# A hybrid encoder layer on one core: where the sigmoids of r and ga and the attention's heads are placed in the weight stream

## Chip, core and metric

The kernel runs on one core of one Trainium2 chip. The metric is the device time of one execution in microseconds; for a program on one core that is the time of this core. The times shown are those of three runs. The profile is of one execution.

## What is computed

One layer: a token mixer and a channel mixer, each with a norm ahead, a norm behind, and scale, shift and gain from a conditioning vector. There are 256 tokens and 2048 features, all in float32. The part that matters here is the token mixer:

```python
def token_mixer(h, w_in, w_a2, b_a2, gla_norm_g, w_out_gla, conv_mix_w, w_out_conv, w_o):
    q, k, v, r, lr, cb, cc, cx, ga, gb = jnp.split(h @ w_in, split_idx, axis=-1)
    log_a = jax.nn.log_sigmoid((lr @ w_a2 + b_a2).astype(jnp.float32)) / GLA_TAU
    o = gla_chunked(heads(q, GLA_DK) * (GLA_DK ** -0.5), heads(k, GLA_DK),
                    heads(v, GLA_DV), heads(log_a, GLA_DK))
    o = rmsnorm(o, gla_norm_g).astype(h.dtype).reshape(bsz, s, GLA_V)
    y_a = (o * jax.nn.silu(r)) @ w_out_gla
    y_b = (cb * causal_dwconv(cc * cx, conv_mix_w)) @ w_out_conv
    m = jax.nn.sigmoid(ga) * y_a + jax.nn.sigmoid(gb) * y_b
    return m @ w_o
```

`gla_chunked` is a linear attention with 4 heads over 4 chunks of 64 frames: a state for each head is decayed by the low-rank gate `log_a` and added to, and every frame reads the state behind its chunk.

## The kernel before

**The weight stream.** All large products go through one list of items, `stream`. A `Chunk` is 256 rows by 512 columns of a weight: one DMA of 512 KB into a buffer `raw` (6 buffers, L275), a rounded copy `whi` on ScalarE (L282, ACT in the profile), the rest `wlo` on VectorE (L291, DVE), and products on TensorE (PE) of `whi` with both parts of the activations and of `wlo` with the high part. In `Feat` (features on partitions, L345) a chunk is 24 matmuls with 256 columns: 16 with `whi`, 8 with `wlo`. A `Gemv` is one tile of 128 x 1024 of `w_ada`, loaded into the same buffers and added to a partial sum on DVE (L438); it uses no PE. `pump(n)` writes out n items of the stream: loads up to 10 items ahead, splits up to 4 ahead, then the item's products. With `each=step_bg` it also runs the generator `bg` one step further behind each `Chunk`, and `run_all(bg)` writes out what is left of it at once.

**Order of execution.** What the program writes out is a text of instructions. The framework then orders the instructions of each engine by a model of the time: the earlier place in the text has the higher priority, but an engine that would be idle in the model takes a later instruction that is ready, and a tile gets a buffer of its tag when one is free (`t2` has 4 buffers, `c4` 2, `g8` 4, the PSUM banks `sm` 2). On the chip each engine then goes through its list in that order.

**The stages around the change**, in the order of the stream, with Gemv items spread between the chunks:

- the last slice of `w_in`'s early columns, `r` among them;
- `cb1` (8 chunks of `w_in`), whose outputs go through `post_cb` (L645, then L633 and L634) into `yb`;
- `w_out_conv` (4 groups of 4 chunks), which reads `yb`; `post_yb` (L653) multiplies by sigmoid(gb);
- `ga` (4 groups of 8 chunks of `w_in`); `post_ga` copies each group to `ga_t` (L677);
- `w_out_gla` (4 groups of 4 chunks), which reads the heads' results `og`, chunk i of a group that of head i; `post_ya` (L806, L807, L633, L634) multiplies by sigmoid(ga) and adds the other branch;
- `w_o` (4 groups of 8 chunks, L400), then the middle of the layer and the channel mixer.

**Background steps beside them.** `gla_gates` runs beside `cb1` and `w_out_conv`, 24 chunks together. It has 21 steps: 4 sigmoids of gb (L662), the split of the low-rank weights (L694, L695), four steps of their product (L699, L700), its copy (L706), two of `w_a2` (L712), log-sigmoid (L716 to L721), the decays of k (L727 to L730), idle ones, and the decay of each chunk of frames, `dtot` (fold, L741, L743). `w_a2` and the low-rank weights each lie in a `t2` buffer from the start to their product.

`gla_heads` runs beside `ga`, 32 chunks. It has 4 steps of SiLU of r (`silus`: sigmoid into a `t2` buffer, L669, and product, L670) and then 8 steps for each of 4 heads: products of k and v (L757); copy and states with `dtot` (L760, L762); nothing; products with q (L771) and squares (L775); their sum over two tiles (L778); sum over partitions on PE (L781); root and reciprocal (L784, L785); norm, gain, SiLU and both parts of the result (L789, L791, L633, L634). That is 36 steps; behind them `gla_then_gates` has the 4 sigmoids of ga (L662 again). So behind ga's last chunk `run_all` writes out the last four steps of head 3 and the four sigmoids together. Then x is loaded again into the buffer that r was in (L1115, two DMAs of SP), and `to_rows` brings the gain vector to a row on every partition (L818, L820, and two DMAs of POOL, L823 and L826) beside the next 6 items.

## Time and profile before

| | us |
|---|---|
| median of three runs | 1462.22 |
| the three runs | 1460.29, 1463.61, 1462.22 |
| span of the profiled execution | 1456.7 |
| PE busy | 1425.5 |
| DVE busy | 1058.4 |
| ACT busy | 816.8 |

The span runs from the first to the last instruction of the profiled execution; the runs' times stand some 5.5 us above it. L12 in a row is line 12 of the kernel; `out<-in` names the tiles without their numbers; a row of a timeline gives start, length, engine, line, operation, tiles, the number of instructions that were merged, and in brackets the idle time of the engine just before with what ended it. The chain of work is followed back from the last instruction. Matmuls are pipelined, so PE counts as busy also where the next matmul is only queued.

### The profile page before, as it was taken

The numbers are of one execution on the slowest core, as the hardware profiler recorded it, in microseconds if no ns is written. First come the engines' busy times: TensorE is split into PE (matmuls) and PEld (weight loads), VectorE is DVE, ScalarE is ACT, GpSimd is POOL, SyncE is SP. The second block draws the span as 40 slices with busy tenths as digits, with TensorE's granted clock in tenths as the row PEclk, the third lists the DMA queues.
The fourth block names the chain that finished last, engine by engine and source line by source line (L and its number), as shares of the span: only waits on it lengthen the run. The fifth ranks groups of instructions, "written<-read, shape, count | busy, mean of one in ns | idle before, by whom it ended". The sixth has DMA issues, their size and how long they took to land.

```text
span 1456.7 us, 23205 instructions
## 1 busy us (share of the span) xinstructions
PE 1425.5 (98%) x9107; PEld 1283.8 (88%) x9107; DVE 1058.4 (73%) x1194; ACT 816.8 (56%) x995; POOL 6.1 (0%) x40
## 2 busy tenths in 40 slices
PE   6999999999999999999999999999999999999997
PEld 6999999898999998988898888888888888888886
DVE  6878777888888777976798767556767645566565
ACT  5789677688564554444665554444545543445453
POOL 0000000000000000000000000000000000000000
PEclk9999999999999999999999999999999999999999
DMA  9999999998978777897467776777776666666552
GB/s 317 332 328 320 360 313 318 343 316 281 337 272 307 248 258 274 305 316 231 135 199 244 224 238 232 248 234 231 229 248 201 215 191 193 183 193 187 188 187 97
DMA packets 177895, 366.82 MB, mean 252 GB/s; under 512 B 13802, under 2 KB 26456, under 8 KB 177017
## 3 DMA queue, kind: packets, MB, share of 16 engines
q1 hardware_dynamic: 176857, 362.17, 75.8%
q0 software_dynamic: 352, 2.11, 0.4%
q8 instruction: 71, 1.16, 0.3%
q10 hardware_dynamic: 576, 1.05, 0.2%
q14 instruction: 39, 0.32, 0.1%
HBM read 363.18 MB, written 2.11 MB: 251 GB/s over the span
## 4 chain that ended last, share of the span: by engine, by line
PE 89%; DMA 4%; DVE 4%; ACT 1%; issue 1%; SPq 0%; DVEq 0%; ACTq 0%
PE mm L345 61%; PE mm L400 27%; DMA raw<-in_w_ada_dram 3%; DVE wlo L291 1%; DMA raw<-in_w_in_dram 1%; ACT whi L282 1%; DVE c L478 1%; DVE c L438 0%; PE sm L1151 0%; DVE t L785 0%; PE sm L757 0%; PE sm L712 0%; DVE g L1059 0%; PE sm L216 0%; DVE raw L208 0%
## 5 line engine op out<-in xcount | busy, mean ns | idle before, releaser
L282 ACT CAST whi<-raw 128x1024 fp32r<-128x1024 f32 (+1 forms) x503 | 512.5, 1024 | 492.8 <-PE mm L345 210.3
L291 DVE TENSOR_TENSOR wlo<-raw,whi 128x1024 fp32r<-128x1024 f32 (+1 forms) x503 | 594.5, 1189 | 260.3 <-ACT whi L282 258.2
L345 PE MATMUL mm<-H,whi 128*128 128x256 f32 (+2 forms) x3712 | 663.2, 322 | 1.2 <-ACT H L253 1.2
L345 PEld LDWEIGHTS mm<-H,whi 128*128 128x128 f32 x3712 | 537.8, 190 | 47.6 <-ACT H L253 1.3
L345 PE MATMUL mm<-H,wlo 128*128 128x256 f32 (+1 forms) x2496 | 377.2, 283 | 0.3 <-DVE wlo L291 0.3
L345 PEld LDWEIGHTS mm<-H,wlo 128*128 128x128 f32 x2496 | 341.7, 190 | 13.2 <-DVE wlo L291 0.7
L400 PE MATMUL mm<-whi,g 128*128 128x512 f32 x704 | 178.9, 393 | 0.0
L400 PEld LDWEIGHTS mm<-whi,g 128*128 128x128 f32 x704 | 132.2, 188 | 28.5
L438 DVE SCALAR_TENSOR_TENSOR c<-raw,sil,c 128x1024 f32<-128x1024 f32 x90 | 115.3, 1281 | 42.0 <-DMA raw<-in_w_ada_dram 41.9
L400 PE MATMUL mm<-whi,H 128*128 128x512 f32 x448 | 119.5, 399 | 0.5 <-ACT whi L282 0.3
L400 PEld LDWEIGHTS mm<-whi,H 128*128 128x128 f32 x448 | 84.5, 191 | 20.2 <-ACT whi L282 1.3
L400 PE MATMUL mm<-wlo,g 128*128 128x512 f32 x352 | 97.6, 391 | 0.0
L478 DVE SCALAR_TENSOR_TENSOR c<-raw,sil,c 128x768 f32<-128x768 f32 (+2 forms) x73 | 78.6, 1076 | 10.0 <-DMA raw<-in_w_ada_dram 9.4
L400 PEld LDWEIGHTS mm<-wlo,g 128*128 128x128 f32 x352 | 66.2, 188 | 14.5
L400 PE MATMUL mm<-wlo,H 128*128 128x512 f32 x224 | 66.1, 397 | 0.0
L438 DVE SCALAR_TENSOR_TENSOR cb<-raw,sil,cb 128x1024 f32<-128x1024 f32 x30 | 38.4, 1281 | 21.5 <-DMA raw<-in_w_ada_dram 21.5
L400 PEld LDWEIGHTS mm<-wlo,H 128*128 128x128 f32 x224 | 42.3, 189 | 9.7
L617 DVE SCALAR_TENSOR_TENSOR t<-pt,fcol,t 128x256 f32<-128x256 f32 x88 | 36.6, 478 | 0.0
L345 PE MATMUL mm<-g,whi 128*128 128x256 f32 x256 | 34.5, 290 | 0.0
L345 PE MATMUL mm<-B,whi 128*128 128x256 f32 x256 | 33.2, 283 | 0.0
L345 PEld LDWEIGHTS mm<-B,whi 128*128 128x128 f32 x256 | 30.7, 188 | 2.6 <-ACT whi L282 2.0
L345 PEld LDWEIGHTS mm<-g,whi 128*128 128x128 f32 x256 | 32.7, 197 | 0.1
(196 smaller groups left out, 736.8 us busy)
## 6 DMA issues: line engine op xcount, KB each, us to landing
raw<-in_w_up_dram SPq DMA_DIRECT2D x176, 512.0 KB, 4.4
raw<-in_w_ada_dram SPq DMA_DIRECT2D x160, 512.0 KB, 5.2
raw<-in_w_in_dram SPq DMA_DIRECT2D x145, 512.0 KB, 5.5
raw<-in_w_down_dram SPq DMA_DIRECT2D x88, 512.0 KB, 4.3
raw<-in_w_o_dram SPq DMA_DIRECT2D x32, 512.0 KB, 5.7
raw<-in_w_ada_dram SPq DMA_DIRECT2D x32, 384.0 KB, 5.5
raw<-in_w_out_conv_dram SPq DMA_DIRECT2D x16, 512.0 KB, 5.5
raw<-in_w_out_gla_dram SPq DMA_DIRECT2D x16, 512.0 KB, 4.8
```

The lines of the kernel that those rows point to most:

```text
L282: nc.scalar.copy(self.hi, self.raw)
L291: nc.vector.tensor_sub(self.lo, self.raw, f(self.hi))
L345: nc.tensor.matmul(out, w[:, t, j * P:(j + 1) * P], x, start=first_in_bank and t == 0 and i == 0, stop=end and t == ch.n - 1 and i == 2, s ...
L400: nc.tensor.matmul(self.out[s], m(c.k0 + t, T)[:, s * P:(s + 1) * P], w[:, t, :], start=first and t == 0 and i == 0, stop=end and t == c.n ...
L438: nc.vector.scalar_tensor_tensor(a, self.raw, sil[:, self.k:self.k + 1], a, op0=ALU.mult, op1=ALU.add)
L478: nc.vector.scalar_tensor_tensor(a, raw, sc, a, op0=ALU.mult, op1=ALU.add)
L617: nc.vector.scalar_tensor_tensor(dst[:, a, :], pt[:, a, i:T + i], w(i, a), dst[:, a, :], op0=ALU.mult, op1=ALU.add)
```

## The change

The four SiLU steps move from the front of `gla_heads` into `gla_gates`, behind gb's sigmoids. The heads alone are then run beside `ga`. The four sigmoids of ga are run beside the next 10 items of the stream, ahead of the two steps of `to_rows`, and no longer ask whether their group is done. The rest of the diff removes comments and docstrings.

```diff
@@ -689,7 +689,8 @@
             nc.sync.dma_start(w_a2b[i * LR:(i + 1) * LR, :], w_a2[0])
         nc.sync.dma_start(w_a2b[2 * LR:, :], b_a2)
         yield from sigmoids(gb_t["t"])
-        # low-rank gate: lr^T, then log_sigmoid(lr @ w_a2 + b) by token
+        yield from silus(sr["t"][:, 0])
+
         w2 = sb([P, KD, 2 * LR], "t2", T2, F32R)
...
@@ -743,7 +744,6 @@
         nc.scalar.activation(dtot, ps[:, 0:16], AF.Exp, scale=1.0 / TAU)
 
     def gla_heads():
-        yield from silus(sr["t"][:, 0])
         kd = qk["t"][:, 1].rearrange("p (s d) -> p s d", s=2)
...
@@ -1103,18 +1103,19 @@
     pump(stream.index(gla_at) + 1 - pos[2], each=step_bg)
     run_all(bg)
 
-    def gla_then_gates():
-        yield from gla_heads()
-        yield from sigmoids(ga_t["t"], lambda g: ga_t["done"] > g)
-
-    bg = gla_then_gates()
+    bg = gla_heads()
     pump(stream.index(gla_to) + 1 - pos[2], each=step_bg)
     run_all(bg)
     xin["t"] = sb([P, 2, D], "XF")
     for s in range(2):
         nc.sync.dma_start(xin["t"][:, s, :], x[0, s * P:(s + 1) * P, :])
-    bg = to_rows("g1", gg1, "g8", G8, og["last"])
-    pump(6, each=step_bg)
+
+    def gates_then_row():
+        yield from sigmoids(ga_t["t"])
+        yield from to_rows("g1", gg1, "g8", G8, og["last"])
+
+    bg = gates_then_row()
+    pump(10, each=step_bg)
     run_all(bg)
```

## The prediction

> **What bounds the kernel now.** I read the page's busy times and its chain first, then TensorE's own waits around the change, then the stages one by one.
>
> ```profile
> PE 1425.5 (98%) x9107; PEld 1283.8 (88%) x9107; DVE 1058.4 (73%) x1194; ACT 816.8 (56%) x995; POOL 6.1 (0%) x40
> ...
> PE 89%; DMA 4%; DVE 4%; ACT 1%; issue 1%; SPq 0%; DVEq 0%; ACTq 0%
> ```
>
> TensorE (PE) is busy for 98% of the span and 89% of the chain lies on it. The change takes no matmul away and adds none, so it can gain only where PE stands still or runs at a lower clock. Which places are those between 380 and 620 us, where everything that the change touches is run? This is the list of PE's waits there, complete (total, times, longest), and the stages in windows: length, then the busy time of PE, PEld, DVE, ACT and POOL with the number of instructions, then PE's granted clock, DMA share and GB/s.
>
> ```profile
> PE sm L781 <- DVE t L778: 2.9, 1, 2.9
> PE sm L781 <- DVE s L869: 0.8, 1, 0.8
> ...
> 404.00:454.00 50.00, 50.00 (x442) 46.85 (x440) 45.00 (x50) 33.88 (x39) 0.00 (x0) 1.00 0.79 270
> 454.00:561.00 107.00, 106.24 (x883) 103.67 (x882) 86.00 (x92) 54.27 (x59) 0.00 (x0) 1.00 0.82 269
> 561.00:612.00 51.00, 48.07 (x398) 47.55 (x398) 43.30 (x51) 24.76 (x28) 1.18 (x2) 0.97 0.83 288
> ```
>
> The rows are the stages of w_out_conv, of ga with the attention's heads, and of w_out_gla. Only two waits exist, both of L781, the matmul that sums a head's squares over the partitions: 0.8 us in ga, 2.9 us in w_out_gla. The second is the fourth head's. Its timeline (start, length, engine, line; in brackets the idle time before and what ended it):
>
> ```profile
> 559.19 1.00 PE L771 MATMUL sm<-g,c 128*128 128x64 f32 x8
> ...
> 561.12 0.60 ACT L775 ACTIVATE t<-sm 128x512 f32<-128x512 f32 x1 [0.72 <-PE sm L771]
> ...
> 562.87 0.28 PE L345 MATMUL mm<-g,wlo 128*128 128x256 f32 x1
> ...
> 564.40 1.28 DVE L438 SCALAR_TENSOR_TENSOR c<-raw,sil,c 128x1024 f32<-128x1024 f32 x1 [2.58 <-DMA raw<-in_w_ada_dram]
> 565.61 0.42 DVE L778 TENSOR_TENSOR t<-t 128x256 f32<-128x256 f32 x1
> ...
> 566.08 0.70 PE L781 MATMUL sm<-t,ones 128*128 128x256 f32 x2 [2.93 <-DVE t L778]
> ```
>
> The squares (L775) are ready at 561.72, but the addition that PE needs (L778) stands on DVE behind L438, which waits 2.58 us for its load. PE has run 17 matmuls of w_out_gla in between, and then its queue is at L781: 2.93 us idle. The idle is followed by a lower clock:
>
> ```profile
> 511.00:514.00 3.00, 2.24 (x19) 2.01 (x17) 1.86 (x4) 2.12 (x2) 0.00 (x0) 1.00 0.81 242
> ...
> 563.00:566.00 3.00, 0.15 (x2) 0.00 (x0) 1.60 (x2) 2.36 (x3) 0.00 (x0) 1.00 0.86 296
> 566.00:569.00 3.00, 2.92 (x17) 2.88 (x18) 0.33 (x2) 1.41 (x2) 0.00 (x0) 0.75 0.73 263
> 569.00:572.00 3.00, 3.00 (x21) 2.94 (x20) 3.00 (x4) 0.84 (x1) 0.00 (x0) 0.68 0.26 62
> 572.00:575.00 3.00, 3.00 (x29) 3.00 (x28) 3.00 (x5) 1.32 (x3) 1.18 (x2) 1.00 0.56 152
> ```
>
> Six microseconds at 0.75 and 0.68 cost 3 x 0.25 + 3 x 0.32 = 1.71 us. The short wait, in the first row, leaves the clock at 1.00. So one place costs 2.93 + 1.71 = 4.64 us.
>
> **The change, part by part.** *The heads.* Before, the attention has 4 steps of SiLU and 4 x 8 steps of heads, 36, for ga's 32 chunks. The last four (L778, L781, L784 and L785, then L789 to L793 of head 3) are written out together behind ga's last chunk, so between L771 and L781 PE has only what w_out_gla offers. Without the SiLU steps the 32 steps fall on 32 chunks: every L781 comes two whole chunks behind its L771, head 3's too. Whether two chunks are enough is read from heads 0 to 2, which have that distance today:
>
> ```profile
> 478.39 1.90 PE L771 MATMUL sm<-g,c 128*128 128x64 f32 x16
> ...
> 485.08 0.42 DVE L778 TENSOR_TENSOR t<-t 128x256 f32<-128x256 f32 x1
> ...
> 485.89 0.59 PE L781 MATMUL sm<-t,ones 128*128 128x256 f32 x2
> ...
> 504.74 1.90 PE L771 MATMUL sm<-g,c 128*128 128x64 f32 x16
> ...
> 513.00 0.42 DVE L778 TENSOR_TENSOR t<-t 128x256 f32<-128x256 f32 x1
> ...
> 532.85 1.90 PE L771 MATMUL sm<-g,c 128*128 128x64 f32 x16
> ...
> 539.19 0.42 DVE L778 TENSOR_TENSOR t<-t 128x256 f32<-128x256 f32 x1
> ```
>
> From L771's start PE comes to L781 after 485.89 - 478.39 = 7.50 us. L778 has ended after 7.11, 8.68 and 6.76 us: in time, late, in time. The late one is the wait of 0.8 us. What was late once is likely to be late again somewhere, since the heads now meet other vectors' loads: I take 0.8 / 3 = 0.27 us for each head, 1.07 for four, against 0.8 now: +0.27 us. Bounds: none late (-0.8), or each as late as the worst seen, 4 x 2.93 (+10.9); the value is that of the nearest rows, the same wait at the same distance. When this stall goes, the next thing that could be late is head 3's result: w_out_gla's fourth chunk reads it, behind three chunks of its own stage.
>
> ```profile
> 540.35 0.59 PE L781 MATMUL sm<-t,ones 128*128 128x256 f32 x2
> ...
> 551.77 0.69 DVE L634 TENSOR_TENSOR g<-t,g 128x512 fp32r<-128x512 f32 x1
> ...
> 606.03 2.05 PE L345 MATMUL mm<-g,whi 128*128 128x256 f32 x16
> ...
> 608.86 2.05 PE L345 MATMUL mm<-g,whi 128*128 128x256 f32 x16
> ```
>
> Head 2 took 552.46 - 540.35 = 12.1 us from L781 to its result. After head 3's L781 PE still has 0.6 us of it, two chunks of ga ((7.50 - 1.90) / 2 = 2.8 us each) and three of w_out_gla (608.86 - 606.03 = 2.83 us each): 14.7 us. So the result is in time by 2.6 us, and I cost it at nothing; a result 4 us later would make PE wait 1.4 us.
>
> *The SiLU of r.* The text moves four steps (one L669 on ACT and one L670 on DVE each) ahead of the low-rank gate. But the planner, not the text, sets where they run:
>
> ```profile
> 437.92 1.67 ACT L669 ACTIVATE t<-XF 128x512 f32<-128x512 f32 x3
> ...
> 448.20 0.69 DVE L670 TENSOR_TENSOR XF<-XF,t 128x512 f32<-128x512 f32 x1
> ...
> 453.75 0.69 DVE L670 TENSOR_TENSOR XF<-XF,t 128x512 f32<-128x512 f32 x1
> ```
>
> They already run beside w_out_conv, though their place in the text is inside ga, which begins at 454 us. They issue no DMA. Moving 4 x 0.69 us of DVE work some 40 to 60 us earlier changes no sum: DVE has 45.00 of 50 us there, and PE shows no wait in that stage. Zero, with the bounds of the buffers in the rivals below.
>
> *The gates, four steps later.* The low-rank product, its log-sigmoid and the decay come four chunks later; 25 steps meet 24 chunks, so the last (L741 to L743, dtot) falls behind w_out_conv's last chunk, and head 0's first product one chunk behind it. Their PE work is only moved. What is queued behind: L762, the states of head 0, and then L771.
>
> ```profile
> 445.32 0.43 PE L741 MATMUL sm<-fold,sel 128*32 128x4 f32 x32
> ...
> 449.94 0.18 ACT L743 ACTIVATE dtot<-sm 128x16 f32<-128x16 f32 x1
> ...
> 468.67 1.14 PE L757 MATMUL sm<-g,g 64*128 64x256 f32 x8
> ...
> 475.41 0.47 DVE L762 SCALAR_TENSOR_TENSOR c<-c,dtot,sm 128x256 f32<-128x256 f32 x1
> ```
>
> From L757 to the last L762's end are 7.2 us, and from L757 to L771 PE takes 478.39 - 468.67 = 9.7 us. dtot takes 4.8 us from L741. After the change L741 is a chunk ahead of L757, so dtot is there at about 2 us behind L757 and the states stay in time: zero, and up to 2 us if ACT is late with dtot.
>
> *ga's sigmoids.* They too run by the planner, not by the text: the text has all four behind ga's last chunk, the trace has the first three inside ga.
>
> ```profile
> 482.24 1.06 ACT L662 ACTIVATE B<-B 128x1024 f32<-128x1024 f32 x1
> ...
> 508.58 1.06 ACT L662 ACTIVATE B<-B 128x1024 f32<-128x1024 f32 x1
> ```
>
> I expect them there again; wherever they are, ACT is busy 54.27 of 107 and 24.76 of 51 us, so nothing. The row of g1 (L818 and two DMAs on POOL's queue) comes four chunks later, and its reader is at the end of w_o's first eight chunks, behind at least 20 us of cover. The reload of x (two DMAs of SP, 1 MB each) waits for head 3's last read of r and so comes about 15 us earlier, to the end of ga; the weight loads behind it on SP are put off as they are today. Zero, up to 2 us if a weight comes late.
>
> **Sum.** -2.93 - 1.71 + 0.27 = -4.4 us. The profiled span of 1456.7 becomes 1452.3; the median of 1462.2 stands 5.5 us above the span, so 1457.8 us. What follows is paced by PE and moves up with it.
>
> [...]
>
> **Rivals.** *Waits come back at the other L781* (0.20). DVE takes its instructions in order, and L438 stands ahead of L778 with waits for loads of up to 2.7 us. If each of four heads loses 0.8 us instead of one: -4.64 + 2.4 = -2.2, 1460.0 us. For it: one in three is late today; against: two are not.
>
> *The clock falls all the same* (0.05). If the dip at 566 to 572 us came from the activity before it and not from the wait, only 2.93 - 0.27 goes: 1459.6 us. Against it: it begins where the wait ends, and ends 6 us later.
>
> *The change does not do what it says* (0.06): the planner puts head 3's tail beside w_out_gla again, as it moved sigmoids and SiLU. Then 1462 us. Against: PE, which is never without work, has followed the text in every head.
>
> *Slower: the four t2 buffers at the end of cb1* (0.14). One holds w_a2 and one the low-rank weights, now four chunks longer; cb's two products and now the four SiLU tiles share the other two. In the rows above a SiLU tile is held from L669 to L670, over 14 us for the last.
>
> ```profile
> 405.83 1.28 DVE L634 TENSOR_TENSOR B<-t,B 128x512 fp32r<-128x512 f32 x2
> ...
> 410.62 1.98 PE L345 MATMUL mm<-B,whi 128*128 128x256 f32 x16
> ```
>
> The product of cb1 is ready at 407.1 and w_out_conv's third chunk needs it at 410.6: 3.5 us of slack. A SiLU tile held 14 us in the way makes PE wait 10.5 us there, and at the clock 1.7 more: 1457.8 + 12.2 = 1470.0. It decides from about 3.5 + 4.4 = 7.9 us of delay. Against it: ahead of cb1's end the products L670 stand early in the text, and DVE would serve them first.
>
> **Chances.** Forecast 0.55, at 1457.8 (its own range 1455.0 to 1459.2: no L781 late, and the spread of the three runs before, up to 1.9 us below the median). About 0.2% (2.9 us) is what a measurement of this kernel can tell from no change. Faster 0.55; the first three rivals are within it, 0.31; slower 0.14. The range goes from 1455.0 to 1463.0: it holds forecast and first three rivals with their scatter, and leaves out the slow one and the far bound of four waits of 2.93 us.
>
> **What would show it.** PE's list of waits without the 2.9 us at L781, clock 1.00 where w_out_gla begins, and w_out_gla in about 46.5 us instead of 51; ga still near 107. L669 ahead of 436 us. Wrong it would be with new waits at L781 or L771 of over 3 us in all, with PE waiting for L634 at w_out_conv's start, or with w_out_gla short of weights.

## The result, and the profile after

The change makes the kernel slower by about a quarter of a per cent: 1464.47 us, median of 20 runs (1461.25 to 1467.99), against 1460.26 us, median of 20 runs of the kernel before on the same chips (1456.53 to 1466.89). The ratio is 1.0027, with a 95% interval of 1.0018 to 1.0037. The forecast of 1457.8 us and its range up to 1463.0 were wrong. Line numbers of the kernel after are used from here on; those of `gla_heads` are the old ones.

The page of the kernel after, busy times and chain:

```profile
PE 1425.5 (97%) x9107; PEld 1281.0 (88%) x9107; DVE 1058.2 (72%) x1194; ACT 815.4 (56%) x994; POOL 6.1 (0%) x40
...
PE 77%; DMA 12%; DVE 8%; issue 2%; ACT 1%; SPq 0%; DVEq 0%; ACTq 0%
```

TensorE does the same work in the same 1425.5 us; what grew is the time that it stands still. The chain shows where to look: 89% of it lay on PE before, 77% now, and DMA and DVE have gone from 4% each to 12% and 8%. So PE now waits for VectorE, and VectorE for loads. The list of PE's waits between 380 and 740 us of the kernel after, largest first (what, total, times, longest):

```profile
PE mm L400 <- DVE wlo L291: 2.9, 2, 1.9
PE sm L1152 <- DVE XF L1138: 2.4, 1, 2.4
PE sm L757 <- DVE t L789: 1.9, 1, 1.9
PE sm L781 <- DVE t L778: 1.6, 1, 1.6
PE mm L345 <- DVE wlo L291: 1.3, 2, 0.9
PE sm L771 <- DVE c L762: 0.7, 1, 0.7
```

The 2.4 us of L1152 belong to the middle of the layer and are there before the change too. The 2.9 us of head 3's L781 in w_out_gla are gone, as meant. In their place stand 0.7, 1.6 and 1.9 us at three of the heads' steps in ga, 1.3 us in w_out_gla and 2.9 us in w_o. The same by stage, in windows of the kernel after cut where the stages begin (w_out_conv, ga, w_out_gla, w_o; the columns are those of the prediction's windows):

```profile
400.44:453.30 52.86, 52.86 (x467) 49.45 (x465) 46.05 (x50) 31.57 (x35) 0.00 (x0) 1.00 0.79 266
453.30:566.14 112.84, 108.36 (x889) 104.73 (x881) 85.06 (x91) 55.10 (x61) 0.00 (x0) 1.00 0.80 255
566.14:612.83 46.69, 45.37 (x396) 44.66 (x394) 39.98 (x48) 20.87 (x25) 1.18 (x2) 1.00 0.85 305
612.83:706.67 93.84, 90.97 (x393) 72.78 (x391) 65.42 (x63) 40.95 (x51) 0.00 (x0) 0.98 0.78 260
```

The kernel before, cut at the same points of its own trace, has 50.04, 106.63, 50.78 and 87.77 us. w_out_conv begins 3.8 us earlier and is 2.8 us longer: three groups of the low-rank product, 24 matmuls, moved into it from the stage ahead. ga is 6.2 us longer, w_out_gla 4.1 us shorter, w_o 6.1 us longer. Together with 0.9 us less behind the mixer that is the difference of the two spans, 1463.0 - 1456.7 = 6.3 us. Of the 6.1 us of w_o some 1.1 are of the cut alone: the last window ends at the first matmul of the middle of the layer (L1152, L1151 before), and five of w_o's matmuls stand behind it before the change and ahead of it after. From its first matmul to its last, w_o takes 89.4 us before and 94.3 after, 4.9 us more. The medians of 20 differ by 4.2 us: the span of the profiled execution lies 3.6 us under the median before and 1.5 us under it after.

**ga.** VectorE's timeline in the kernel after, at heads 0 and 1, and PE's two longest waits there (start, length, engine, line, tiles; in brackets the idle time before and what ended it):

```profile
473.55 1.28 DVE L438 SCALAR_TENSOR_TENSOR c<-raw,sil,c 128x1024 f32<-128x1024 f32 x1 [2.67 <-DMA raw<-in_w_ada_dram]
474.75 1.22 DVE L291 TENSOR_TENSOR wlo<-raw,whi 128x1024 fp32r<-128x1024 f32 x1
475.88 0.42 DVE L778 TENSOR_TENSOR t<-t 128x256 f32<-128x256 f32 x1
478.54 1.28 DVE L438 SCALAR_TENSOR_TENSOR c<-raw,sil,c 128x1024 f32<-128x1024 f32 x1 [2.24 <-DMA raw<-in_w_ada_dram]
479.74 2.36 DVE L291 TENSOR_TENSOR wlo<-raw,whi 128x1024 fp32r<-128x1024 f32 x2
483.40 1.28 DVE L438 SCALAR_TENSOR_TENSOR c<-raw,sil,c 128x1024 f32<-128x1024 f32 x1 [1.30 <-DMA raw<-in_w_ada_dram]
484.60 1.74 DVE L785 RECIPROCAL t<-t 128x256 f32<-128x256 f32 x1
486.26 1.16 DVE L291 TENSOR_TENSOR wlo<-raw,whi 128x1024 fp32r<-128x1024 f32 x1
487.34 0.68 DVE L789 TENSOR_TENSOR t<-sm,t 128x512 f32<-128x512 f32 x1
...
476.36 0.70 PE L781 MATMUL sm<-t,ones 128*128 128x256 f32 x2 [1.59 <-DVE t L778]
488.16 1.10 PE L757 MATMUL sm<-g,g 64*128 64x256 f32 x6 [1.94 <-DVE t L789]
```

Head 0's small additions (L778, 0.42 us) stand in VectorE's queue behind a multiply-add L438 that waits 2.67 us for its tile of w_ada. Two more late loads, 2.24 and 1.30 us, delay L785 and L789. L789 is the last reader of one of the two small PSUM banks, and head 1's products (L757) need that bank: so a late load of a vector that has nothing to do with the attention stops TensorE twice. It is the mechanism of the stall before the change, at other heads.

**w_o.** The kernel after again, around PE's longest wait there:

```profile
621.43 1.28 DVE L438 SCALAR_TENSOR_TENSOR c<-raw,sil,c 128x1024 f32<-128x1024 f32 x1 [2.21 <-DMA raw<-in_w_ada_dram]
622.63 1.28 DVE L806 TENSOR_TENSOR t<-mm,B 128x512 f32<-128x512 f32 x2
623.83 1.28 DVE L807 TENSOR_TENSOR t<-t,A 128x512 f32<-128x512 f32 x2
625.03 1.22 DVE L291 TENSOR_TENSOR wlo<-raw,whi 128x1024 fp32r<-128x1024 f32 x1
626.30 1.18 PE L400 MATMUL mm<-wlo,H 128*128 128x512 f32 x4 [1.91 <-DVE wlo L291]
```

The weight's low part (L291) is late by the same kind of load, 2.21 us, and by the four operations of the last group of w_out_gla. The windows of this place show what followed:

```profile
626.00:629.00 3.00, 2.70 (x9) 2.15 (x10) 3.00 (x5) 2.61 (x3) 0.00 (x0) 0.74 0.44 154
629.00:632.00 3.00, 3.00 (x11) 2.41 (x10) 3.00 (x3) 1.05 (x1) 0.00 (x0) 0.69 0.80 240
```

Six microseconds at 0.74 and 0.69 cost 3 x 0.26 + 3 x 0.31 = 1.71 us more. So the 4.1 us that w_out_gla gave back are paid again, in ga and in w_o.

### The profile page after: what moved, and what is told of

The parts are those of the page before. It is cut to its first block, busy times and chain, and to the rows that moved or that the text cites. A ratio compares the mean times of both kernels' runs of the same rounds, so it can differ in the third digit from the quotient of the medians.

```text
span 1463.0 us, 23211 instructions
## 1 busy us (share of the span) xinstructions
PE 1425.5 (97%) x9107; PEld 1281.0 (88%) x9107; DVE 1058.2 (72%) x1194; ACT 815.4 (56%) x994; POOL 6.1 (0%) x40
## 4 chain that ended last, share of the span: by engine, by line
PE 77%; DMA 12%; DVE 8%; issue 2%; ACT 1%; SPq 0%; DVEq 0%; ACTq 0%
PE mm L345 50%; PE mm L400 26%; DMA raw<-in_w_ada_dram 7%; DMA raw<-in_w_in_dram 2%; DVE wlo L291 2%; DVE c L438 1%; DMA raw<-in_w_out_conv_dram 1%; DVE c L478 1%; ACT whi L282 1%; DMA raw<-in_w_out_gla_dram 1%; DMA raw<-in_w_o_dram 0%; DVE g L617 0%; DVE raw L208 0%; DVE t L785 0%; DVE fold L210 0%
## 5 line engine op out<-in xcount | busy, mean ns | idle before, releaser
L291 DVE TENSOR_TENSOR wlo<-raw,whi 128x1024 fp32r<-128x1024 f32 (+1 forms) x503 | 594.6, 1189 | 259.4 <-ACT whi L282 256.3
L345 PE MATMUL mm<-H,whi 128*128 128x256 f32 (+2 forms) x3712 | 663.5, 322 | 1.6 <-ACT H L253 1.2
L345 PEld LDWEIGHTS mm<-H,whi 128*128 128x128 f32 x3712 | 536.9, 189 | 49.0 <-issue 1.7
L345 PE MATMUL mm<-H,wlo 128*128 128x256 f32 (+1 forms) x2496 | 376.4, 282 | 1.5 <-DVE wlo L291 1.5
L345 PEld LDWEIGHTS mm<-H,wlo 128*128 128x128 f32 x2496 | 341.1, 189 | 14.3 <-DVE wlo L291 1.7
L438 DVE SCALAR_TENSOR_TENSOR c<-raw,sil,c 128x1024 f32<-128x1024 f32 x90 | 115.3, 1281 | 51.2 <-DMA raw<-in_w_ada_dram 51.2
L438 DVE SCALAR_TENSOR_TENSOR cb<-raw,sil,cb 128x1024 f32<-128x1024 f32 x30 | 38.5, 1282 | 21.9 <-DMA raw<-in_w_ada_dram 21.9
L345 PE MATMUL mm<-B,whi 128*128 128x256 f32 x256 | 33.2, 282 | 0.0
L345 PEld LDWEIGHTS mm<-B,whi 128*128 128x128 f32 x256 | 30.9, 188 | 1.8 <-issue 1.5
L345 PE MATMUL mm<-g,whi 128*128 128x256 f32 x256 | 32.1, 278 | 0.0
L345 PEld LDWEIGHTS mm<-g,whi 128*128 128x128 f32 x256 | 30.5, 188 | 0.0
```

The source lines that it names most:

```text
L291: nc.vector.tensor_sub(self.lo, self.raw, f(self.hi))
L345: nc.tensor.matmul(out, w[:, t, j * P:(j + 1) * P], x, start=first_in_bank and t == 0 and i == 0, stop=end and t == ch.n - 1 and i == 2, s ...
L438: nc.vector.scalar_tensor_tensor(a, self.raw, sil[:, self.k:self.k + 1], a, op0=ALU.mult, op1=ALU.add)
```

## The experiments

The theory at the start: VectorE takes its queue in order (above, L778 stands behind an L438 that waits 2.67 us), multiply-adds with late loads stand in it, and the change only moves the place where such a wait meets a step that PE needs; for w_o, theory B named the reload of x, which comes earlier, and its rival C the row of g1, which comes later. The other rivals: the moved SiLU or sigmoids cost the time by themselves; or the late loads are new. Every ratio is to the kernel before, run beside it on the same chip.

**The SiLU alone, the tail alone.** In the first run the heads and the SiLU are those of the change, and behind ga stands the old text; in the second it is the other way round.

```diff
-    bg = gla_heads()
+    def gla_then_gates():
+        yield from gla_heads()
+        yield from sigmoids(ga_t["t"], lambda g: ga_t["done"] > g)
+
+    bg = gla_then_gates()
...
-    bg = gates_then_row()
-    pump(10, each=step_bg)
+    bg = to_rows("g1", gg1, "g8", G8, og["last"])
+    pump(6, each=step_bg)
```

> The SiLU steps move, ga's sigmoids and the row of g1 stay at their old place in the text. Theory A (the heads, four chunks earlier, have their small VectorE steps queued behind multiply-adds that wait for w_ada's loads): ga keeps the waits of the changed kernel, some 4.5 us, and ga stays near 113 us. Theory B (x's reload and the stage's loads take what the removed stall had given the loads) expects the wait at w_o's start to stay too, about 4.6 us with the clock, so some 1464 us. Rival C (the row of g1, four chunks later, is what crowds the loads at the end of w_out_gla): the wait at w_o's start goes, about 1460 us.

> Only ga's sigmoids and the row of g1 move; the heads keep their 36 steps. Theories A and B: ga near 106.6 us, the stall of 2.9 us and the low clock behind it at w_out_gla's second chunk stay, and nothing new at w_o: the time of the kernel before, about 1460 us. Rival C: a wait of 3 us or more at w_o's start, about 1464 us.

The SiLU alone: 1460.77 us, ratio 1.0002 (0.9989 to 1.0014). Its ga is 110.7 us, with 2.2 us of wait at head 1's L757 and 0.2 at L781; w_out_gla is 45.6 us and w_o 89.3 us, both without a wait. The tail alone: 1459.95 us, ratio 0.9991 (0.998 to 1.0003). Its w_out_gla is 53.1 us, with one wait of 5.35 us at head 3's L781, and w_o 87.8 us. So neither half alone makes the kernel slower, and the wait at w_o needs both: the heads that end early, and the row of g1 that comes late. Theory B alone missed, since in the first run x is reloaded as early as in the changed kernel (569.0 us, against 571.1) and w_o is quiet; rival C alone missed in the second. ga's waits, 2.7 us with the smaller ones, are fewer than the 4.5 us of theory A. Up to the end of ga, PE, VectorE, ScalarE and the queue of SP have the same list of instructions here as in the changed kernel, so this difference is one between executions.

**The reload of x held back.** The changed kernel, with x's two DMAs behind a load of a weight of w_o; they are issued at 633 us, 17 us into that stage.

```diff
+    pump(n_mixer - 36 - pos[2])
+    last_load = [ch for ch in stream[:pos[0]] if isinstance(ch, Chunk)][-1].load
     xin["t"] = sb([P, 2, D], "XF")
     for s in range(2):
-        nc.sync.dma_start(xin["t"][:, s, :], x[0, s * P:(s + 1) * P, :])
+        with tc.issue_after(last_load.ins):
+            nc.sync.dma_start(xin["t"][:, s, :], x[0, s * P:(s + 1) * P, :])
```

> The changed kernel with x's reload held behind a load in the middle of w_o. Theory B: w_out_gla stays near 46.7 us and the wait at w_o's start (2.9 us, and 1.7 us of low clock) goes, about 1460 us; ga keeps its waits. If the loads of w_out_gla and w_o are late for another reason (rival C, or too many items in the stage): no change, about 1464 us.

1460.8 us, ratio 1.0005 (0.999 to 1.0019). The wait at w_o falls from 2.9 to 0.4 us and w_o from 93.8 to 89.6 us; w_out_gla has 45.6 us with 1.3 us of wait for a low part; ga keeps its waits (2.2 us at L781, 1.9 at L757, 0.6 at L771) and has 114.5 us.

**ga's multiply-adds left out.** The loads stay, so that the traffic is the same; the multiply-adds with w_ada in ga are left out, so the vectors made of them lack those tiles.

```diff
                 a = gemv_acc[self.c0]
-                nc.vector.scalar_tensor_tensor(
+                if not self.in_ga:
+                  nc.vector.scalar_tensor_tensor(
                     a, self.raw, sil[:, self.k:self.k + 1], a, op0=ALU.mult, op1=ALU.add)
```

> The changed kernel without the multiply-adds of w_ada's tiles that fall in ga (19 or 20 of 1.28 us; their loads stay, so three of the conditioning vectors are incomplete). Theory A: with nothing on VectorE that waits for these loads, the waits at L757, L771 and L781 in ga go and ga takes about 107 us instead of 113, the time falls by 5 us or more. Rival D (the heads begin too close behind the gates, or the two small PSUM banks are short): waits of some 4 us stay in ga.

1454.79 us, ratio 0.9955 (0.9939 to 0.9971). The window of its ga (columns as above):

```profile
453.87:560.08 106.21, 106.21 (x891) 103.89 (x881) 65.02 (x72) 55.07 (x61) 0.00 (x0) 1.00 0.81 266
```

PE is busy in all of ga's 106.21 us: no wait is left. The DMA share is 0.81, as in the kernel after with 0.80. The waits of ga come from these operations on VectorE; whether from their place in its queue or from their work, this run can't tell. The wait at w_o stays, with 2.4 us, so it is a matter of its own.

**The row of g1 first.** The changed kernel with the two generators behind ga exchanged.

```diff
     def gates_then_row():
-        yield from sigmoids(ga_t["t"])
         yield from to_rows("g1", gg1, "g8", G8, og["last"])
+        yield from sigmoids(ga_t["t"])
```

> The changed kernel with one thing put back: behind ga the row of g1 is started first and ga's sigmoids follow, so that its steps (the copy of L820, then the broadcast of L826) stand four chunks earlier in the queues, as before the change. The order of everything up to w_out_gla stays. Theory (the row's place behind late loads, with x's reload beside them, makes w_o wait): both waits of w_o's matmuls for the low parts (L400 <- L291, 2.9 us together) go, the stage of w_o falls from 93.8 to 89.3-90 us as where only the SiLU had moved, ga stays at 110.5-113 us, and the time is 1459.5-1461.5 (ratio 0.999-1.001). Rival (x's reload alone, or ga's sigmoids, which run elsewhere, make it): the waits at w_o stay, the stage stays at 92 or above, and the time is 1463.5-1465.5 (ratio 1.002-1.0035).

1462.39 us, ratio 1.0016 (1.0001 to 1.0031): between the two expectations. w_out_gla has 45.6 us and no wait, w_o 90.6 us with one wait of 1.5 us instead of two of 2.9 together: about half of the wait at w_o, and the low clock behind it (the granted clock is 1.00 from 611 to 626 us), have gone with the row's place. ga, whose text is that of the change, took 115.1 us in this execution, against an expected 110.5 to 113.

**The heads four chunks later, and two.** Empty steps ahead of the heads put them where they stood before the change (four), or half way (two).

```diff
     def gla_heads():
+        for _ in range(4):
+            yield
```

> The changed kernel with four empty steps ahead of the heads, so that every head's step stands at the chunk at which it stood before the change; the SiLU stays beside w_out_conv and the tail stays changed. Theory (each head's small VectorE steps stand in order behind multiply-adds that wait for their w_ada loads, and only where they fall among them decides which wait shows): ga falls from 112.8 to 106.5-108.5 us with under 1.2 us of PE waits, and head 3's wait for L778 of 2.5-5.7 us is back in w_out_gla, whose stage is 49-53 us; the time stays at 1462-1466. Rival (ga lost time because the SiLU, or the matmuls that moved out of cb1, leave its loads later, whatever the heads' place): ga stays at 110.5-113 us with 2.7-4.7 us of waits.

> The changed kernel with two empty steps ahead of the heads: they stand two chunks later than in the changed kernel and two earlier than before. Theory (only the place among the late multiply-adds decides): VectorE's idle time before L438 in ga stays at 17-21 us, the PE waits are at other heads' steps than in the changed kernel (none at the same step of the same head), ga lies between 106.5 and 115 us with the waits in step, and head 3's end lies at ga's end or just behind it; no prediction of the sum closer than 1457-1466. Rival (the changed kernel's ga is slow for another reason than the heads' place): the waits stay at head 0's L778 and head 1's products, 4 us or more in ga, time 1463-1466.

Four: 1461.99 us, ratio 1.0016 (1.0003 to 1.0029). PE's waits (lines are two higher than in the kernel after: L783 is L781, L780 is L778):

```profile
PE sm L783 <- DVE t L780: 3.8, 2, 3.1
```

and the windows of its ga and w_out_gla:

```profile
453.28:561.31 108.03, 106.58 (x888) 103.46 (x879) 84.43 (x90) 53.67 (x59) 0.00 (x0) 1.00 0.82 269
561.31:610.98 49.67, 45.82 (x397) 45.01 (x397) 40.59 (x49) 23.80 (x27) 1.18 (x2) 1.00 0.81 281
```

ga is back at 108.0 us, and head 3's wait is back in w_out_gla. The stalls moved with the heads, while the SiLU, the sigmoids and the row stand as in the change. The profiled execution, 1459.14 us, is the fastest of this kernel's ten, so the stages don't show why its median is 1.7 us above that before. The next three rows tell why the stalls move: VectorE's L438 in the window from 450 to 556 us, in the kernel before, after, and with four empty steps (count, busy time, mean ns, then the idle time before them).

```profile
L438 DVE SCALAR_TENSOR_TENSOR c<-raw,sil,c 128x1024 f32<-128x1024 f32 x21 | 26.9, 1283 | 19.2 <-DMA raw<-in_w_ada_dram 19.2
```

```profile
L438 DVE SCALAR_TENSOR_TENSOR c<-raw,sil,c 128x1024 f32<-128x1024 f32 x19 | 24.4, 1283 | 20.7 <-DMA raw<-in_w_ada_dram 20.6
```

```profile
L438 DVE SCALAR_TENSOR_TENSOR c<-raw,sil,c 128x1024 f32<-128x1024 f32 x20 | 25.7, 1283 | 20.5 <-DMA raw<-in_w_ada_dram 20.5
```

VectorE loses 19 to 21 us to late loads of w_ada in all three. The change did not make them later. It costs PE something only where a step of a head stands behind such a load, and that is a matter of place. Two empty steps: 1462.41 us, ratio 1.0012 (0.9999 to 1.0025), the idle time before L438 23.3 us, ga 113.3 us. Here the expectation of the theory was partly wrong: the waits are at the same steps as in the kernel after, as the rival had it, 2.2 us at head 0's sum and 0.9 at head 1's products, only 5 us later, with 1.5 us more at head 2's sum. Each of the first two stands behind other late loads: two L438 that waited 2.90 and 1.23 us stand ahead of head 0's sum, and two that waited 0.96 and 3.16 us ahead of its root. With the end of head 3 two chunks later, its result was late for w_out_gla, 2.2 us at L345 for `g` (L633): the slack that the prediction had worked out (2.6 us with the heads ending in ga) is used up there.

**Five multiply-adds moved from ga into cb1 and w_out_conv.**

```diff
-SHARE = [20, 15, 20, 10]
+SHARE = [20, 20, 15, 10]
```

> The changed kernel with five of ga's 20 multiply-adds with w_ada moved into w_out_conv, and five of w_out_gla's 20 ... 15 in ga, 20 in w_out_conv, w_out_gla as before with 10. Theory (heads behind late multiply-adds): one of them for every 2.1 chunks of ga in place of 1.6, so that ga's PE waits fall from 4.5 to 0-2.5 us and ga to 106.5-110 us; w_out_conv, which has the DMA share of 0.7-0.96 in the changed kernel, takes five more loads of 0.5 MB without waits of over 1 us; w_o's waits stay; time 1459-1463. Rival (loads late because the DMA engines cannot bring more): w_out_conv's stage grows by 2 us or more and ga's waits stay above 3 us; time 1464-1467.

1460.76 us, ratio 1.0002 (0.9987 to 1.0016). 16 instead of 19 multiply-adds fall into the window from 450 to 556 us, the idle time before them is 21.1 us as ever, and ga has 111.3 us, just above the 106.5 to 110 expected, with one wait of 2.6 us, now at head 3's products. w_out_conv has 52.5 us, so it takes its share of them without loss. Three multiply-adds fewer, with the same idle time before them, did not take the wait away.

**A seventh buffer for raw weights.** If the loads are late because six buffers hold them back, a seventh lets each start an item earlier. First everywhere, then only from cb1 to the mixer's end (and for one load at 25 us), in the kernel after and in the kernel before.

```diff
-RAW_BUFS, SPLIT_BUFS, LOOK_SPLIT, LOOK_DMA = 6, 4, 4, 10
+RAW_BUFS, SPLIT_BUFS, LOOK_SPLIT, LOOK_DMA = 7, 4, 4, 10
```

```diff
+    def raw_buf():
+        i = pos[0]
+        if x_lo[0] <= i < x_hi[0] and (i - x_lo[0]) % 7 == 6:
+            return "rawx", 1
+        return "raw", RAW_BUFS
...
-            self.raw = sb([P, KT, NC], "raw", RAW_BUFS)[:, 0:self.n, :]
+            self.raw = sb([P, KT, NC], *raw_buf())[:, 0:self.n, :]
...
-            while pos[0] < min(len(stream), i + 1 + look_dma) and pos[0] < pos[1] + RAW_BUFS:
+            while (pos[0] < min(len(stream), i + 1 + look_dma)
+                   and pos[0] < pos[1] + RAW_BUFS + (x_lo[0] <= pos[0] < x_hi[0])):
...
+    x_lo[0], x_hi[0] = stream.index(early_to) + 1, n_mixer
```

> The changed kernel with seven buffers for raw weights in place of six, which lets each load start one item earlier. Theory (the multiply-adds wait because six buffers hold their loads back, the DMA engines being only 0.75-0.89 busy in ga): VectorE's idle time before L438 in ga falls by half or more, ga's PE waits from 4.5 to under 1.5 us, ga to 106.5-108.5 us, and in w_out_gla and w_o, where the share is 1.00, little changes; time 1457-1461. Rival (the DMA engines set the landing, not the buffers): the same idle before L438, ga 110-113 us, time 1463-1466. The planner's order changes too with the buffer, which may move the waits to other heads.

> The changed kernel with a seventh buffer for raw weights from the item behind the first 5120 columns of w_in to the mixer's end only (every seventh load of this stretch goes into it); before and after that stretch six buffers and the order of the engines as in the changed kernel. Theory (the multiply-adds wait because six buffers hold their loads back): as with seven buffers everywhere, PE waits between 400 and 690 us under 1.5 us in all, ga 106.5-108, w_out_gla 45-46, w_o 88-90 us; and without the 9.7 us that seven buffers everywhere cost behind the mixer: span 1449-1453, time 1451-1456 (ratio 0.994-0.997). Rival (with seven everywhere ga was quiet because the planner's order had changed from the start on, and not because loads came earlier): ga stays at 110-115 us with 2.7-5 us of waits and the time at 1460-1465.

> The kernel before the change with the same seventh buffer in the same stretch. Theory (head 3's wait in w_out_gla, too, is a small VectorE step behind a multiply-add whose load is late): its wait for L778 falls from 2.9 us to under 1 us and the stage of w_out_gla from 50.8 to 45-47.5 us; with ga at 106-108 the time is 1453-1457, within 0.2% of the changed kernel with the same buffer: where loads come in time the change has nothing left to gain. Rival (head 3's wait comes of the heads' end lying in w_out_gla, as the prediction had it): the wait of 2.5 us or more and a stage of 49 us or more stay, and the changed kernel with the seventh buffer is 4 us or more faster than this one.

Everywhere: 1458.07 us, ratio 0.9984 (0.9971 to 0.9996). PE has no wait of over 0.3 us between w_out_conv and the middle of the layer: ga 107.5, w_out_gla 45.2, w_o 88.9 us. But the idle time before L438 in ga is 19.0 us, not half of 20.7: the loads are as late as before, and the quiet ga must come of something else; the planner's order of ga is another here, and the last pair of runs says more on it. Behind the mixer the new order costs 9.7 us (766.0 instead of 756.4 us to the end), with 5.4 us of PE's waits for L974 and 3.4 us of low clock (0.93 in the window from 690 to 740 us) that the kernel after doesn't have there (1.00). In the one stretch only, the idle time falls to 15.3 us (11.6 and 3.7 before the multiply-adds of the two kinds of buffer); w_out_gla and w_o are quiet, 45.2 and 88.9 us, but ga has three waits of 0.9, 1.3 and 1.8 us, a granted clock of 0.50 behind the last (519 to 525 us), and 115.2 us: 1461.69 us, ratio 0.9999 (0.9988 to 1.001). In the kernel before it is slower, 1466.86 us, ratio 1.0031 (1.0015 to 1.0048), with two waits of 8.7 us together at L781's place; there the idle time before L438 is 25.3 us, more than without the buffer. Both expectations of the theory missed: the buffer doesn't reliably make the loads earlier, and where they wait less, the waits that are left can still meet a head.

**The multiply-adds of ga on GpSimd.** Out of VectorE's queue, with the work kept.

```diff
                 a = gemv_acc[self.c0]
-                nc.vector.scalar_tensor_tensor(
+                if self.in_ga:
+                    nc.gpsimd.tensor_scalar_mul(self.raw, self.raw, sil[:, self.k:self.k + 1])
+                    nc.gpsimd.tensor_add(a, a, self.raw)
+                else:
+                  nc.vector.scalar_tensor_tensor(
                     a, self.raw, sil[:, self.k:self.k + 1], a, op0=ALU.mult, op1=ALU.add)
```

> The changed kernel with ga's multiply-adds with w_ada taken off VectorE: each is two operations on GpSimd (a product in place in the raw buffer, then the sum), the loads and the rest as in the changed kernel. GpSimd stands idle in ga, and its time for 128x1024 is in no trace so far. Theory (the heads' small steps wait in VectorE's queue behind multiply-adds whose loads are late): with the load's wait on another queue, VectorE's idle time before L438 in ga and the PE waits of 4.5 us in ga go, ga is 106-107.5 us as where these multiply-adds were left out; w_o's waits stay; time 1456.5-1460 (ratio 0.997-0.9995). Rival (what helped there was the work left out, VectorE's 1.28 us each and the buffers' sooner release, and not whose queue waits): the buffers are held for the longer two steps of GpSimd, weights' loads come later, the PE shows waits of over 3 us at the weights' low or high parts (L345 <- L291 or L282) or at the heads, and the time is 1463 or more.

1503.49 us, ratio 1.0286 (1.0266 to 1.0307). Its groups on GpSimd in the whole span, and VectorE's splits in the window from 460 to 560 us:

```profile
L440 POOL TENSOR_SCALAR raw<-raw,sil 128x1024 f32<-128x1024 f32 x19 | 64.3, 3385 | 126.3 <-ACT whi L282 96.3 <-DMA raw<-in_w_ada_dram 21.5 <-DVE wlo L291 8.4
L441 POOL TENSOR_TENSOR c<-c,raw 128x1024 f32<-128x1024 f32 x19 | 47.8, 2517 | 1.6
...
L291 DVE TENSOR_TENSOR wlo<-raw,whi 128x1024 fp32r<-128x1024 f32 x22 | 35.1, 1603 | 34.1 <-ACT whi L282 33.1 <-PE sm L786 0.8
```

A multiply-add takes 3.39 + 2.52 = 5.9 us there, against 1.28 on VectorE, and 19 of them fill 112 us. GpSimd is busy for 100.3 of the 153.6 us that ga takes. The theory's 1456.5 to 1460 us missed widely, since a multiply-add is so much longer there; between queue and work this decides nothing.

**The seventh buffer from the first item on.** The stretch of the seventh buffer begins with the stream, so that the mixer's order is drawn anew, and the order of VectorE and ScalarE behind it stays that of the kernel after; then the same in the kernel before.

```diff
-    x_lo[0], x_hi[0] = stream.index(early_to) + 1, n_mixer
+    x_lo[0], x_hi[0] = 0, n_mixer
```

> The changed kernel with the seventh buffer from the first item of the stream to the mixer's end, so that the planner's order of the mixer is drawn anew, as where all of the kernel had seven, while behind the mixer the order of the changed kernel stays (VectorE's and ScalarE's orders there are the same). Theory (the loads are as late as ever, VectorE idle 17-21 us before L438 in ga in every run so far, and only which steps stand behind them decides): idle before L438 in ga 11-21 us whatever the PE waits are; ga anywhere from 106.5 to 115 us with PE waits of 0-4.5 us in step with it; behind the mixer 755-759 us and not 766; w_out_gla 45-46, w_o 88-90. Time 1450-1461 by ga's draw. Rival (seven buffers from the start make the loads early, which made ga quiet): idle before L438 under 10 us and ga at 106-108 with under 0.5 us of waits; time 1449-1453.

> The kernel before the change with the seventh buffer from the first item of the stream to the mixer's end, as in the run of the changed kernel that gave 1453.14 us. It tells whether that gain belongs to the buffer alone or needs the change. If the buffer alone gives it: the stretch ahead of w_out_conv falls from 404.2 to 399.5-401 us (the changed kernel had 400.4 and 396.8 without and with the buffer), w_o stays at 87.8, ga and w_out_gla move with the draw of the planner's order, 106.5-113 and 45-54 us; time 1453-1460. If the change is needed: head 3's wait in w_out_gla stays at 2.5 us or more, that stage at 49 us or more, and the time is 1456-1462, 3 us or more behind the changed kernel with the same buffer.

The kernel after with it: 1453.14 us, ratio 0.9944 (0.9931 to 0.9957), the fastest of all. The kernel before with it: 1453.63 us, ratio 0.9943 (0.9928 to 0.9959). The two are the same. Their PE waits of the heads, the changed kernel first (here L765 is L757, L797 is L789, L793 is L785, L446 is L438, L789 is L781, L786 is L778):

```profile
PE sm L765 <- DVE t L797: 2.3, 1, 2.3
```

```profile
PE sm L789 <- DVE t L786: 4.4, 1, 4.4
```

With the change the wait lies in ga (113.1 us, then w_out_gla 45.2 and w_o 88.9); without it in w_out_gla (ga 106.5, w_out_gla 52.3, w_o 87.8). In both, w_out_conv begins earlier, at 396.8 and 399.3 us instead of 400.4 and 404.2. So the buffer is worth 0.6% by itself, and the change is worth nothing beside it: it trades one stall for another of nearly the same price (ga and w_out_gla together take 158.3 us with the change and 158.8 without).

The changed kernel with this buffer also tells queue from work. VectorE's order in ga is there that of the run with seven buffers everywhere, but for two multiply-adds and a split. One of the two stands directly ahead of head 0's root (first two rows); with seven buffers everywhere it stands behind L789 (last two rows), and no wait of a head is over 0.2 us:

```profile
477.26 1.28 DVE L446 SCALAR_TENSOR_TENSOR c<-raw,sil,c 128x1024 f32<-128x1024 f32 x1 [0.63 <-DMA raw<-in_w_ada_dram]
478.47 1.74 DVE L793 RECIPROCAL t<-t 128x256 f32<-128x256 f32 x1
```

```profile
478.44 0.68 DVE L789 TENSOR_TENSOR t<-sm,t 128x512 f32<-128x512 f32 x1
479.04 1.28 DVE L438 SCALAR_TENSOR_TENSOR c<-raw,sil,c 128x1024 f32<-128x1024 f32 x1
```

The same multiply-add, with the same work, puts 0.63 + 1.28 = 1.9 us ahead of the step in one place and nothing in the other; PE waits 2.3 us in the one kernel and not in the other. The multiply-add ahead of it, too, was later in the first (2.64 us of idle time, against 1.19), so the place is not all of the 2.3 us.

## Why the prediction was wrong

**What bounds the kernel, and the stall to be removed: right.** PE has 1425.5 us of work in both. The wait of 2.93 us at head 3's L781 and the 1.71 us of low clock behind it are gone; w_out_gla took 46.69 us, for which the prediction said about 46.5. The change does what it says, and head 3's result was in time: no wait for it stands in w_out_gla.

**The term that failed: "0.8 / 3 = 0.27 us for each head", +0.27 us for the waits in ga.** Measured: 0.7 + 1.6 + 1.9 + 0.3 = 4.5 us of waits in ga, against 0.8 before, +3.7 us. Of the 6.2 us that ga grew, 0.7 more are head 3's two matmuls of L781, which now lie in ga, and some 1.8 are in no row of a wait. The step counted how often one sort of wait (L781) had been seen, at the heads' old places, and gave it to the new places as an average. But the rows that the prediction quoted already held the cause: L438 with waits of 2.58 us for its load, ahead of L778. VectorE loses about 20 us to such loads in ga. Every step of a head that falls behind one is late, L762 and L789 as well as L778, and L789 stops the next head's products by the bank that it frees: this the prediction had not looked at. The rival "waits come back at the other L781" had the right mechanism, with too small a price (2.4 us) and at one line of three.

**The second: x's reload and the row of g1, "Zero, up to 2 us if a weight comes late".** Measured: 2.9 us of waits and 1.71 us of low clock in w_o, which from its first matmul to its last grew by 4.9 us. The step argued from each reader's cover, "at least 20 us" for the row. The reader was indeed covered. What was late were the weights. The order of events is in these windows of w_out_gla, kernel after:

```profile
581.00:586.00 5.00, 5.00 (x45) 5.00 (x44) 3.68 (x6) 1.61 (x2) 0.00 (x0) 1.00 1.03 398
586.00:591.00 5.00, 4.55 (x39) 4.35 (x38) 5.00 (x8) 2.66 (x4) 0.63 (x1) 1.00 0.32 122
591.00:596.00 5.00, 5.00 (x49) 4.85 (x50) 5.00 (x6) 0.49 (x1) 0.56 (x1) 1.00 0.75 238
596.00:601.00 5.00, 5.00 (x44) 4.86 (x43) 3.57 (x6) 2.15 (x4) 0.00 (x0) 1.00 1.01 389
601.00:606.00 5.00, 4.13 (x36) 3.93 (x35) 4.97 (x7) 2.23 (x3) 0.00 (x0) 1.00 1.03 390
```

x's 2 MB, issued at 571 us, have landed by 581 us, and with the loads queued beside them the DMA engines are full up to 586 us (share 1.03, the column before the last); an L438 at 582.3 us waits 3.76 us for its load; then VectorE is busy without a gap, the raw buffers are held (the queue of SP waits 6.8 us for an L291) and the share falls to 0.32; and when the loads run again, the row's 1 MB (L826 at 591.2 us) goes with them, at shares of 1.01 and 1.03 up to 606 us. With the row first L826 is issued at 583.4 us instead of 591.2. Taking back the one (89.6 us) or the other (90.6 us) takes most of the loss away. And the stall that was removed seems to have been the time in which both were hidden: with four empty steps the stall is back, and w_o is at 87.8 us with the text of x and the row as the change has it.

**At nothing, and rightly so:** the SiLU, which ran ahead of 406 us (L669 at 385.6 to 402.9 us), the gates and dtot, and ga's sigmoids, of which the planner put three inside ga (L662 at 490.9, 514.1 and 542.3 us) and one into w_out_gla. w_out_conv shows no wait, so the slow rival of the four t2 buffers did not come about: the kernel is slower for another reason.

**"What follows is paced by PE and moves up with it": wrong,** as w_o shows. The rest behind the mixer did move (757.3 and 756.4 us to the end), but there chance has a hand in it: behind the wait at L1152 (L1151 before) the granted clock was 0.50 from 704.01 to 707.42 us before, and 1.00 after.

**The offset.** The sum stood on a median 5.5 us above the profiled span, from three runs; with 20 it is 3.6 us. That made the forecast 2.0 us too high, against the direction of the error. The 5.5 us are no fixed cost: where a run has both figures, its time is 1.7 or 1.8 us above its own span, and the rest is that the profiled execution was a fast one.

**The clock.** The second rival, that the clock falls all the same, is refuted for its place: w_out_gla has 1.00 throughout. But that the wait of 2.93 us had 1.71 us of low clock behind it was not a matter of its length alone. With the tail alone, where PE, VectorE and ScalarE have the same lists as before the change up to 570 us, the wait was 5.35 us, and the two matmuls of L781 behind it took 1.22 us, against 0.70 before the change; with four empty steps a wait of 3.10 us at the same place was followed by no low clock (1.00 in w_out_gla). The last section has more of such waits.

What stays open: why the loads of w_ada come late, by some 18 to 23 us together in ga wherever the heads stand. The engines of DMA are 0.8 busy there, and with a seventh buffer the idle time before L438 was between 12.8 and 25.3 us, not nothing. Nor is it shown which of the 4.9 us of w_o belong to x and which to the row, since the two together cost more than either.

## What to carry to other kernels

A stall that comes of a queue taken in order is not removed by moving the step that suffers from it: look for what stands ahead in the queue (here 19 multiply-adds in ga, seven of which wait 1.3 to 3.6 us for their load), and count every step that can fall behind it, with the buffers that this step frees. Traffic that a stall had hidden comes out when the stall goes (here, it seems, the 4.9 us of w_o); a change that shortens a stage must be priced with the transfers of that stage in the time that is left. And such waits are a draw: with the same list of instructions on every engine ga took 110.7 to 115.1 us in four profiled kernels here, and a new order by the planner is another draw, so an edit's worth is read against a control that has everything else (here the buffer with and without the change).

## What was not expected of the hardware

**A longer wait did not always cost more clock.** A wait of some 2 us cost sometimes nothing beyond itself, sometimes 1.7 us, sometimes 3.4 us of lower clock. Worked out from the granted clock in windows, as at w_o above:

| kernel, wait | lost us |
|---|---|
| before, 2.93 at head 3's L781 | 1.71 |
| after, 1.91 in w_o | 1.71 |
| two empty steps, 2.22 at head 0's L781 | 1.71 |
| x late, 1.90 at head 1's L757 | 1.68 |
| row first, 2.70 at head 1's L757 | 3.42 |
| seventh buffer in a stretch, 1.81 | 3.39 |
| seventh buffer from the start, 2.33 | 3.39 |
| after, 1.59 and 1.94 in ga | 0 |
| SiLU alone, 2.19 in ga | 0 |
| five multiply-adds moved, 2.63 in ga | 0 |
| four empty steps, 3.10 at head 3's L781 | 0 |

A wait of 1.81 us lost 3.39 us here, and one of 3.10 us lost nothing. Two of the rows are at the same place, head 3's L781: first the kernel before, then the one with four empty steps (the second number is PE's busy time, the granted clock is the third from the end):

```profile
564.07:567.48 3.41, 1.40 (x10) 1.35 (x11) 1.62 (x2) 1.97 (x4) 0.00 (x0) 1.00 0.83 287
567.48:570.89 3.41, 3.41 (x18) 3.35 (x18) 2.19 (x2) 0.74 (x1) 0.00 (x0) 0.50 0.35 129
```

```profile
561.62:565.04 3.42, 1.94 (x17) 1.74 (x15) 1.27 (x3) 3.37 (x4) 0.00 (x0) 1.00 0.99 292
565.04:568.45 3.41, 1.78 (x13) 1.73 (x14) 1.57 (x2) 1.81 (x3) 0.00 (x0) 1.00 0.79 273
568.45:571.86 3.41, 3.41 (x31) 3.41 (x31) 2.69 (x2) 1.41 (x2) 0.00 (x0) 1.00 0.31 105
```

Before the change PE stands still for 2.01 us of the first window, and the granted clock is 0.50 in the second. With four empty steps it stands still for 1.48 and 1.63 us of the first two, and the clock is 1.00 in all three. In the middle of the layer a wait of 2.4 us (L1151 before, L1152 after) has 0.50 behind it, from 704.01 to 707.42 us, in the kernel before, and 1.00 in the kernel after. What decides whether such a wait lowers the clock is not shown by these runs.

**GpSimd beside VectorE.** In the run with the multiply-adds of ga on GpSimd, a product of 128x1024 by a column took 3.39 us there and a sum of two such tiles 2.52 us. In the kernel after, VectorE's multiplication of that shape by a column (L435) took 0.75 us and its subtraction of two such tiles (L291) 1.21 us. The product is the longer of the two on GpSimd and the shorter on VectorE. Spans on GpSimd are rough in a profile, but a pair of the two operations took 464.61 to 470.87 us, 6.3 us. And VectorE's own L291 went from 1.21 to 1.60 us beside it.
